# Loading and transposing half of the next x tiles during the second product, two blocks ahead

## The chip, the cores and the metric

The kernel runs on one core of a Trainium2 chip. The metric is the device time of one execution in microseconds (us). Each time below is a median over several executions. Verdicts are ratios with a 95% interval: the mean time of one kernel's fast runs over the mean of the other's fast runs in the same rounds, so not quite the ratio of the quoted medians.

## The reference, cut to what matters

```python
batch, m, k, h, n = 16, 512, 768, 3072, 768
y = np.matmul(x, w1) + b1                      # "first product"
y = 0.5 * y * (1.0 + erf(y / np.sqrt(2.0)))    # gelu
return np.matmul(y, w2).astype(np.float32)     # "second product"
```

The 8192 rows of x are worked off in 8 blocks of 1024 rows, numbered 0 to 7. A block has 8 row tiles of 128 rows.

## The kernel before

The kernel replaces 8 block multiplications by 7 (a Strassen scheme), twice nested in the second product. From block 2 on, every block is 12 "units" of the first product and 7 "units" of the second, each unit with seven products. Four parts matter here.

From block 2 on, all loads that the tensor engine waits for go through the queue of the sync engine (SP), in program order: first-layer weights (`w1s`, 672 KB a unit), second-layer weights into a ring of ten buffers (`w2s`, 288 KB a product), and the transposes of x (SBUF to SBUF). The loads of x go through the GpSimd (POOL) queue, with most stores of the output.

```python
def load_ring(sb, n):                    # second-layer weights of product n
    if n < 49 and sb < nsb:
        nc.sync.dma_start(out=ring_of(sb, n), in_=w2s[w2_order[n]][:])

def xh_of(sb, t):
    ...                                  # from block 2 on: three buffers for loaded x tiles
    return xh_late[t % 3]

def load_x(sb, t):
    xhs[t] = xh_of(sb, t)
    nc.gpsimd.dma_start(out=xhs[t], in_=xr[:, sb * 8 + t, :])

def transpose_dma(sb, t):
    nc.sync.dma_start_transpose(out=xT_of(sb, t), in_=xhs[t])

class Unit3:                             # a unit of the second product
    def mm(self, q, dst, first, c0, c1, ts=(0, 1)):
        n = w2_at[self.p, q]
        w = ring_of(self.sb, n)
        ...                              # 12 matmuls of 192 columns with w
        load_ring(self.sb, n + RING)     # RING = 10: refill the buffer just used
```

Between the products of a unit, "fill" functions issue everything else. This is the one of the first product (`k` is the unit, `slot` the place in it):

```python
def fill_mm1(sb, k, slot):
    ...
    if slot == 3 and sb + 1 < nsb:
        if 1 <= k < 9:
            load_x(sb + 1, k - 1)
        if 3 <= k < 11:
            transpose_dma(sb + 1, k - 3)
    if slot == 5:
        if k + 3 < NH and n + 3 not in wts:
            load_wt(n + 3)               # first-layer weights, three units ahead
        if k >= 3:
            for m in range(2 * (k - 3), min(2 * (k - 2), RING)):
                load_ring(sb, m)         # the first ten of the ring
```

The transposed x has two buffers, for even and odd blocks. So block `sb + 2`'s buffer is free as soon as block `sb`'s first product is done.

## Time and profile before

Median 855.0 us of six executions (854.53 to 856.19).

| what | number | view |
|---|---|---|
| tensor engine (PE) busy | 845.9 of 854.0 us | page, part 1 |
| granted clock | 0.999 | cores |
| one first-product unit, unstalled | 4.53 us | timeline, from start to start |
| one second-product unit, unstalled | 6.93 us | timeline |
| one block, unstalled | 12 x 4.53 + 7 x 6.93 = 102.9 us | |

The page of the kernel before: busy time of each engine, DMA share in 40 slices, and the chain of work that ended last.

```profile
PE 845.9 (99%) x6407; PEld 566.5 (66%) x6407; DVE 667.5 (78%) x1128; ACT 423.9 (50%) x688; POOL 83.7 (10%) x135
...
DMA  9996987659989698996989889897998969967397
...
PE 96%; DMA 3%; POOL 0%; issue 0%; DVE 0%
```

The tensor engine is the limit, and the DMA engines are nearly as busy. PE busy alone would not say that the matmuls run at their best rate. The unit times do: 4.53 us / 21 = 215.7 ns for a matmul of 512 columns, which is the 215.7 ns that the Trainium skill, page "TensorE: Matmul & The Clock Gate", section "Wait — 56ns, not 53.3ns?", gives for back-to-back matmuls of this size. So nothing but the few DMA pieces of the chain can be gained. One of them, in block 3's first product (chain in order of time: start, length, what):

```profile
371.52 1.25 PE bX L379 x6
372.77 9.93 DMA arena<-w1s
382.70 0.05 issue
382.75 0.82 PE bX L379 x3
```

The piece is as long as the load took from issue to landing (9.93 us). The tensor engine did not stand that long: it worked on earlier units for most of it, and the start-to-start gaps show 1.33 us of stall here and 0.33 us at 376.

The windows view of before by stage; after the times come the busy time (and count) of PE, PEld, DVE, ACT and POOL, then the granted clock, the DMA share and GB/s. The rows are block 3's first product, block 3's second, block 4's first, block 4's second.

```profile
343.00:397.30 54.30, 52.96 (x306) 28.07 (x304) 39.06 (x75) 39.52 (x62) 2.66 (x5) 1.00 0.95 241
397.30:445.00 47.70, 47.70 (x527) 43.73 (x525) 44.78 (x69) 11.02 (x21) 6.01 (x9) 1.00 0.91 326
446.00:500.30 54.30, 54.30 (x314) 29.06 (x313) 39.58 (x76) 40.65 (x64) 3.13 (x6) 1.00 0.94 254
500.30:548.00 47.70, 47.70 (x526) 43.75 (x525) 44.65 (x69) 10.42 (x21) 6.05 (x9) 1.00 0.91 320
```

Read the last two columns: both kinds of stage are above 0.9 in DMA share. The first product moves fewer GB/s at a higher share, because of small packets: in the first row the transposes (256 B, 35 ns a packet) and the x loads (1536 B, 148 ns) are 24% of the bytes and 45% of the packet time.

### The profile page before, as it was taken

To read this page: it belongs to the slowest core of one execution; us is meant where nothing else is said; L and a number is where in the kernel's file an instruction comes from. 1 tells how busy PE (TensorE), PEld (TensorE's weight loads), DVE (VectorE), ACT (ScalarE), POOL (GpSimd) and SP (SyncE) were. 2 spreads that over 40 slices of the span, in tenths; PEclk is the share of its full clock that TensorE was granted. 3 is DMA by queue.
4 is the path that set the end of the run, shared out by engine and by line. 5 is a ranking of instruction groups with operands and counts; after the bars stand their busy time and mean duration, and the time that the engine had idled before them with its cause. 6 is when DMAs were issued, how large, how long until landed. Compare 5 with 4: busy or idle time off the path is not lost.

```text
span 854.0 us, 16428 instructions
## 1 busy us (share of the span) xinstructions
PE 845.9 (99%) x6407; PEld 566.5 (66%) x6407; DVE 667.5 (78%) x1128; ACT 423.9 (50%) x688; POOL 83.7 (10%) x135
## 2 busy tenths in 40 slices
PE   8999999999999999999999999999999999999998
PEld 4444445687544897448974499645995469944798
DVE  5856678786657998669976799667996689957997
ACT  5777762122277513874138722477216771267611
POOL 5021100002100002000020000200012000010000
PEclk9999999999999999999999999999999999999999
DMA  9996987659989698996989889897998969967397
GB/s 226 235 232 89 256 165 269 240 194 216 234 225 291 212 321 293 265 287 228 333 287 271 254 275 334 274 339 158 313 347 264 307 170 333 348 218 266 101 304 286
DMA packets 143522, 219.05 MB, mean 256 GB/s; under 512 B 61756, under 2 KB 84724, under 8 KB 143444
## 3 DMA queue, kind: packets, MB, share of 16 engines
q1 hardware_dynamic: 117968, 179.83, 65.7%
q0 software_dynamic: 25440, 38.15, 21.1%
q8 instruction: 50, 0.82, 0.4%
q14 instruction: 28, 0.23, 0.1%
q10 hardware_dynamic: 36, 0.01, 0.0%
HBM read 180.30 MB, written 47.87 MB: 267 GB/s over the span
## 4 chain that ended last, share of the span: by engine, by line
PE 96%; DMA 3%; POOL 0%; issue 0%; DVE 0%
PE bY L379 21%; PE bY L484 15%; PE bX L379 14%; PE bX L484 10%; PE bZ L379 7%; PE bW L379 7%; PE bZ L484 5%; PE bW L484 5%; PE bY L423 5%; DMA arena<-w1s 2%; PE bZ L423 2%; PE bX L423 2%; PE bW L423 2%; DMA arena<-in_x_dram 1%; PE bY L571 1%; PE bX L571 1%
## 5 line engine op out<-in xcount | busy, mean ns | idle before, releaser
L189 DVE TENSOR_TENSOR arena<-arena 128x1536 f16<-128x1536 f16 (+7 forms) x632 | 403.5, 669 | 6.5 <-PE bW L423 1.1
L379 PEld LDWEIGHTS <-arena 128*128 128x128 f16 x1995 | 194.2, 98 | 229.6 <-DMA arena<-w1s 3.9
L484 PEld LDWEIGHTS <-arena 128*128 128x128 f16 x3528 | 292.1, 98 | 8.3 <-issue 0.3
L379 PE MATMUL bY<-arena 128*128 128x512 f16 x855 | 216.7, 379 | 0.0
L604 DVE TENSOR_TENSOR arena<-bY,arena 128x512 f32<-128x512 f32 (+1 forms) x103 | 70.1, 680 | 130.1 <-PE bY L379 89.6
L379 PE MATMUL bX<-arena 128*128 128x512 f16 x570 | 140.4, 379 | 1.5 <-DMA arena<-w1s 1.5
L597 ACT COPY bY<-bX 128x512 f32<-128x512 f32 (+1 forms) x144 | 79.2, 550 | 120.7 <-DVE arena L533 87.3
L484 PE MATMUL bY<-arena 128*128 128x192 f16 x1500 | 138.3, 246 | 0.0
L395 ACT ACTIVATE arena<-arena,b1t 128x1024 f16<-128x1024 f32 x95 | 109.2, 1149 | 54.8 <-DVE arena L632 54.8
L617 ACT COPY arena<-bW 128x512 f32<-128x512 f32 (+1 forms) x148 | 81.6, 552 | 91.5 <-PE bW L484 43.5
L484 PE MATMUL bX<-arena 128*128 128x192 f16 x1020 | 93.1, 246 | 0.0
L632 DVE TENSOR_TENSOR arena<-bZ,arena 128x512 f32<-128x512 f32 (+1 forms) x103 | 70.0, 679 | 22.8 <-PE bZ L379 18.8
L379 PE MATMUL bZ<-arena 128*128 128x512 f16 x285 | 77.0, 379 | 0.0
L379 PE MATMUL bW<-arena 128*128 128x512 f16 x285 | 77.0, 379 | 0.0
L423 PEld LDWEIGHTS <-arena 128*128 128x128 f16 x528 | 51.6, 98 | 34.1 <-issue 0.2
L400 ACT ACTIVATE arena<-bX,b1t 128x512 f16<-128x512 f32 x95 | 64.7, 681 | 10.4 <-PE bX L379 10.3
L516 POOL DMA_DIRECT2D out_dram<-arena x42 | 30.6, 728 | 395.1 <-DVE arena L628 358.6
L400 ACT ACTIVATE arena<-bY,b1t 128x512 f16<-128x512 f32 x95 | 64.0, 674 | 0.0
L648 ACT COPY bZ<-bY 128x512 f32<-128x512 f32 (+1 forms) x54 | 29.0, 537 | 65.5 <-DVE arena L632 30.5
L294 POOL DMA_DIRECT2D arena<-in_x_dram x60 | 32.5, 546 | 260.9 <-DMA arena<-arena 152.9
L650 DVE COPY bZ<-bY 128x512 f32<-128x512 f32 (+1 forms) x63 | 43.5, 691 | 6.3 <-DVE arena L632 0.5
L484 PE MATMUL bZ<-arena 128*128 128x192 f16 x504 | 48.5, 246 | 0.0
(60 smaller groups left out, 392.3 us busy)
## 6 DMA issues: line engine op xcount, KB each, us to landing
arena<-w2s SPq DMA_DIRECT2D x294, 288.0 KB, 4.7
arena<-w1s SPq DMA_DIRECT2D x72, 672.0 KB, 6.4
out_dram<-arena POOLq DMA_DIRECT2D x42, 384.0 KB, 5.4
w2s<-arena SPq DMA_DIRECT2D x49, 288.0 KB, 3.1
arena<-in_x_dram POOLq DMA_DIRECT2D x60, 192.0 KB, 6.8
w1s<-arena SPq DMA_DIRECT2D x12, 672.0 KB, 8.1
arena<-in_w_dram POOLq DMA_DIRECT2D x17, 384.0 KB, 8.5
out_dram<-arena SPq DMA_DIRECT2D x17, 384.0 KB, 3.4
```

Of the source, the lines that this page charges most:

```text
L189: nc.vector.tensor_tensor(out=o, in0=a, in1=b, op=op)
L294: nc.gpsimd.dma_start(out=xhs[t], in_=xr[:, sb * 8 + t, :])
L379: nc.tensor.matmul(out=dst[:, 0:RH], lhsT=w1_op(self.wt, slot)[:, c, :], rhs=a[:, c, :], start=first and c == 0, stop=c == self.C - 1, ski ...
L395: nc.scalar.activation(out=self.G[1][:, hi, :, :], in_=self.tmp, func=GELU, bias=b1t[:, 2 * hi + 1:2 * hi + 2])
L400: nc.scalar.activation(out=self.G[0][:, hi, row, :], in_=bank[:, 0:RH], func=GELU, bias=b1t[:, 2 * hi:2 * hi + 1])
L423: nc.tensor.matmul(out=dst[:, 0:N2], lhsT=a, rhs=w[:, :, c, :], start=first and c == 0, stop=c == self.C - 1, skip_group_check=True)
L484: nc.tensor.matmul(out=dst[:, t * N4:(t + 1) * N4], lhsT=a, rhs=w[:, c, :], start=first and c == 0 and t == ts[0], stop=c == NQ - 1, skip_ ...
L597: nc.scalar.copy(out=bY[u.g % 2][:, 0:u.F], in_=bX[u.g % 2][:, 0:u.F])
L604: nc.vector.tensor_tensor(out=u.c22(), in0=bY[u.g % 2][:, 0:u.F], in1=w[:, 0:u.F], op=ADD)
L617: nc.scalar.copy(out=w[:, 0:u.F], in_=bW[:, 0:u.F])
L632: nc.vector.tensor_tensor(out=u.c12(), in0=bZ[:, 0:u.F], in1=w[:, 0:u.F], op=ADD)
L650: nc.vector.tensor_copy(out=bZ[:, 0:u.F], in_=bY[u.g % 2][:, 0:u.F])
```

## The change

Its evident intent is to take DMA work out of the first product, where weights arrive late. For blocks 4 to 7, tiles 0 to 3 are loaded and transposed during the second product two blocks back, and tiles 4 to 7 stay in the first product at every other unit. Block 3 is fed as before.

```diff
             if slot == 3 and sb + 1 < nsb:
-                if 1 <= k < 9:
-                    load_x(sb + 1, k - 1)
-                if 3 <= k < 11:
-                    transpose_dma(sb + 1, k - 3)
+                ts = range(8) if sb == ONE else (4, 4, 5, 5, 6, 6, 7, 7)
+                if 1 <= k < 9 and (sb == ONE or k % 2):
+                    load_x(sb + 1, ts[k - 1])
+                if 3 <= k < 11 and (sb == ONE or k % 2):
+                    transpose_dma(sb + 1, ts[k - 3])
@@ the second product's fill @@
+            if sb + 2 < nsb and slot == 4:
+                if k < 4:
+                    load_x(sb + 2, k)
+                if 2 <= k < 6:
+                    transpose_dma(sb + 2, k - 2)
```

## The prediction

> **What bounds the kernel.** TensorE. The page gives PE 845.9 us busy of 854.0 (99%), the chain of waits is 96% PE, the granted clock is 0.999. By the timeline a first-product unit takes 4.53 us (21 matmuls of 512 columns) and a second-product unit 6.93 us (84 of 192), so a block needs 12 x 4.53 + 7 x 6.93 = 102.9 us. Blocks 4 to 6 take 102.97 to 103.15 us: nothing is left to gain there. Block 3 takes 104.68. The chain has two pieces "DMA arena<-w1s" of 9.8 and 9.9 us, one in block 2 (258.9, before the changed part), one in block 3 (372.8 to 382.7). Gaps between matmul starts in block 3 are 0.33 us at 376 and 1.33 us at 381: 1.7 us, for late first-layer weights. That is all the change can win.
>
> **What it moves.** Sixteen tiles (4 each for blocks 4 to 7) go from the first product of the block before to the second product two blocks back. No matmul, vector or scalar work changes. Per tile the trace shows a load (128 packets of 1536 B, 134 ns each under load: 1.1 us of all 16 DMA engines) and a DMA transpose (768 packets of 256 B, 18 to 19 ns alone, up to 79 ns crowded: 0.9 to 1.5 us), and 1.2 us of the SP queue.
>
> **First product.** The windows view gives DMA share 0.95 in block 3's first product, 0.93 to 0.94 in later ones. Weight loads there land 7 to 10 us after issue. Half the transposes, at every other unit, relieves this: I expect block 3's 1.7 us gone. The three x buffers come free early, so three of the four moved loads should issue near the end of the first product, where DMA is nearly idle (before: nothing at 488 to 492 us).
>
> **Second product.** This is the risk. DMA share is 0.90 to 0.91, but 0.96 to 1.03 in the middle units: a 288 KB ring load per 0.99 us product (0.75 us of DMA when packets take 93 ns) plus stores. A ring load is issued when product n ends and is needed 9 products later, 8.9 us. Its latency is 3 to 5 us, with a peak of 5.8 to 6.9 in unit 3 (blocks 2 to 5). Transposes come in units 2 to 5. The first should be absorbed; the second, with the fourth tile's load, adds 2 to 2.6 us just at the peak, the third about 1. Latency should reach 8 to 9.5 us: up to about 1 us of stall per block, in four blocks. I estimate 0 to 4 us, most likely 1.5.
>
> The Trainium skill, page "DMA: Bandwidth & Descriptors", section "Issuing engines are not separate DMA queues", says that all issuers end on the same 16 engines and interleave; the trace agrees (weight loads slow beside x loads and transposes), so moving work shifts it only.
>
> **Sum.** -1.7 + 1.5: about 855.0 us, range 852.8 to 859.5. Faster by over 2% is practically excluded, as PE idles under 1%; slower by over 2% would need over 4 us of stall in each of four blocks.
>
> **What would show it.** Right: no "w1s" piece at 372 us in the chain; block 3 at 103.0 us; DMA share of the changed first products about 0.8, second products near 1.0; ring loads (arena<-w2s) landing 2 to 3 us later in units 3 and 4. Wrong: PE waiting for arena<-w2s by several us per block.
>
> **What would make it wrong.** Transposes costing ring loads more than 1.5 us each; an in-order SP queue held by a transpose whose x load is late; first-product weights still late in block 3.

## The result, and the profile after

856.52 us median (855.54 to 858.19) against 855.0 us. The ratio is 1.0019, interval 1.0006 to 1.0032. Executions over 1.5% slower than the fastest of the same kernel are left out of the means. Two more sets of the same kernel, below, gave 1.0017 (0.9992 to 1.0042) and 0.9999 (0.9984 to 1.0014). So by the three ratios the change costs something between nothing and two tenths of a per cent (the widest interval reaches 0.42%), and two of the three sets cannot tell it from zero.

The same lines of the page after:

```profile
PE 845.8 (99%) x6407; PEld 566.3 (66%) x6407; DVE 667.8 (78%) x1128; ACT 423.3 (50%) x688; POOL 83.7 (10%) x135
...
DMA  9995987659999899986999789996999939967397
...
PE 95%; DMA 4%; SPq 0%; ACT 0%; issue 0%; DVE 0%
```

The same four stages in the windows view after:

```profile
343.00:397.30 54.30, 54.30 (x313) 28.91 (x311) 39.59 (x76) 41.09 (x65) 2.68 (x6) 1.00 0.88 235
397.40:445.10 47.70, 47.70 (x526) 43.75 (x525) 44.77 (x69) 11.03 (x21) 6.55 (x10) 1.00 1.07 340
446.10:500.40 54.30, 54.30 (x314) 29.04 (x313) 39.60 (x76) 40.60 (x64) 2.57 (x5) 1.00 0.86 236
500.40:548.10 47.70, 46.99 (x522) 43.28 (x520) 44.75 (x69) 9.60 (x19) 5.69 (x9) 1.00 1.06 328
```

The first products fell from 0.95 and 0.94 to 0.88 and 0.86 in DMA share, the second ones rose from 0.91 to 1.07 and 1.06. (Packet times can overlap, so a share can exceed 1.) The piece at 372 us is gone from the chain, and another has come in the second product of block 4:

```profile
518.27 0.57 PE bY L484 x7
518.85 8.99 DMA arena<-w2s
527.84 0.05 issue
527.89 1.16 PE bZ L484 x12
```

A ring load is needed 9 products after its issue, 9 x 0.99 = 8.9 us. This one took 8.99 us and was issued about 0.5 us after its turn (the loads before the transpose left every 0.99 us, the last at 515.33, so its turn was 518.30), behind a transpose on the queue; the stall was 0.87 us. The waits of the SP queue for a DMA to land show a kind that is absent before. Its largest line in the total:

```profile
SPq L283 <- DMA arena<-w2s: 10.5, 21, 1.8
```

The columns are us in total, times and longest. The trace has the SP queue's DMAs, transposes included, use eight completion semaphores (the signals that a DMA has landed) in turn. So the ninth DMA may have to wait for the first to land; that this is the reason for these waits is inferred.

To see where the stalls lie without the noise of the start, I measure each block by the time from its first ring refill (the eleventh ring load) to that of the next block. Without stalls this is 102.97 us. It holds the second product of the one block and the first product of the next. Ring latency, from issue to landing, is taken over the same refills: the first ten loads of a block, issued in its first product, can take longer (up to 10.2 us before) and have more time.

| profile | 2 to 3 | 3 to 4 | 4 to 5 | 5 to 6 | 6 to 7 | largest ring latency, blocks 2, 3, 4, 5 |
|---|---|---|---|---|---|---|
| before | 104.68 | 102.97 | 102.99 | 102.97 | 102.98 | 6.4, 6.2, 6.9, 5.8 |
| after | 103.46 | 102.98 | 103.87 | 103.05 | 102.99 | 8.8, 7.9, 9.2, 8.0 |

The 1.71 us in the first row is a wait for first-layer weights, the 0.49, 0.90 and 0.08 in the second are waits for the ring: 1.7 us gained, 1.5 us paid. (Block 2's first product, which the change does not touch, stalled by 0.5 us in the one profile and by 1.8 us in the other. That is why the profiled span of the changed kernel is the longer one, 854.8 against 854.0, although this balance is slightly in its favour.)

### The profile page after: what moved, and what is told of

It is laid out like the page before. It is cut to its first block, busy times and chain, and to the rows that moved or that the text cites. A ratio compares the mean times of both kernels' runs of the same rounds, so it can differ in the third digit from the quotient of the medians.

```text
span 854.8 us, 16436 instructions
## 1 busy us (share of the span) xinstructions
PE 845.8 (99%) x6407; PEld 566.3 (66%) x6407; DVE 667.8 (78%) x1128; ACT 423.3 (50%) x688; POOL 83.7 (10%) x135
## 4 chain that ended last, share of the span: by engine, by line
PE 95%; DMA 4%; SPq 0%; ACT 0%; issue 0%; DVE 0%
PE bY L379 21%; PE bX L379 14%; PE bY L484 14%; PE bX L484 9%; PE bW L379 7%; PE bZ L379 7%; PE bY L423 5%; PE bZ L484 5%; PE bW L484 4%; DMA arena<-w2s 2%; PE bZ L423 2%; PE bW L423 2%; PE bX L423 2%; PE bY L571 1%; DMA arena<-w1s 1%; DMA arena<-in_w_dram 1%
## 5 line engine op out<-in xcount | busy, mean ns | idle before, releaser
L400 ACT ACTIVATE arena<-bX,b1t 128x512 f16<-128x512 f32 x95 | 64.7, 681 | 10.4 <-PE bX L379 10.3
```

The costliest lines, as they stand in the source:

```text
L400: nc.scalar.activation(out=self.G[0][:, hi, row, :], in_=bank[:, 0:RH], func=GELU, bias=b1t[:, 2 * hi:2 * hi + 1])
```

## The experiments

Theory A: both kinds of stage lie at the edge of a deadline of about 9 us (first-layer weights in the one, ring loads in the other), and the DMA engines' time for x uses up the margin wherever it is put. Rival B: not the DMA engines' time matters but the in-order SP queue, which stands while a transpose waits or is being issued. Rival C: the stalls are chance, and the change does nothing.

### The two kernels again

before_again:

> The kernel before, unchanged, to see how much the stalls of TensorE vary from run to run. Theory A (the change trades a first-product stall of 1.7 us in block 3 for second-product stalls of about 1.3 us, and the rest of the measured difference is spread): the block 3 stall for first-layer weights is there again, 1 to 2.5 us, no stall for ring loads; the stall in block 2's first product, which the change does not touch, differs from the 0.5 us of the first profile. Rival C (the block 3 stall itself is chance): it is absent or under 0.5 us. Time 855.0.

after_again:

> The changed kernel again. Theory A: no stall for first-layer weights in block 3, ring-load stalls of 0.5 to 3 us in all in the second products of blocks 2 to 5; time 856.5. Rival C: the ring-load stalls of 0.46 and 0.87 us are gone, and what differs lies before block 2's second product.

after_third:

> The changed kernel a third time, for the size of its small loss and for a third look at where it stalls. The two sets so far have it 0.19% and 0.17% slower, the second not clear of zero. Theory A (the second products of blocks 2 to 5 now lie at the edge, so a stall of 0.3 to 1 us comes in some block of some executions, as the first products' did before): largest ring-load latency 7.5 to 9.2 us in blocks 2 to 5 and 5.4 to 7.1 in blocks 6 and 7, stalls of 0 to 2 us in all there, last weight load of blocks 3 to 5 within 8 us, time 855 to 856.5 us. If the loss of the first set was chance: within 0.05% of before.

| profile | 2 to 3 | 3 to 4 | 4 to 5 | 5 to 6 | 6 to 7 | largest ring latency, blocks 2, 3, 4, 5 |
|---|---|---|---|---|---|---|
| before_again | 102.99 | 102.97 | 104.40 | 102.97 | 102.98 | 6.2, 6.6, 6.3, 5.9 |
| after_again | 102.98 | 102.97 | 102.99 | 102.96 | 102.99 | 8.0, 7.6, 8.2, 7.6 |
| after_third | 103.38 | 102.98 | 103.00 | 102.98 | 103.00 | 8.4, 8.0, 8.6, 7.8 |

Times: before_again 855.37 us (its own ratio to the kernel before, the same kernel, 1.0005, 0.9989 to 1.0021), after_again 855.34 us, after_third 855.13 us. The expectation for block 3 failed: the weight stall was not there, it was in block 5. The chain of before_again shows it, and the SP queue's timeline shows what stood before the load:

```profile
577.20 0.85 PE bX L379 x4
578.05 10.05 DMA arena<-w1s
588.10 0.05 issue
```

```profile
572.70 0.32 SPq L216 DMA_DIRECT2D arena<-w1s  x1
573.07 1.32 SPq L283 DMA_DIRECT2D arena<-w2s  x2
575.87 2.09 SPq L300 DMA_TRANSPOSE arena<-arena  x1
578.05 0.76 SPq L216 DMA_DIRECT2D arena<-w1s  x1
```

The first two columns are the start and the length of what stands on the queue: from 574.39 the transpose stood at its head, waiting for its x tile, which landed at 575.85. Then its issue took 2.09 us, and the weight load left 5.35 us after the one before it instead of 4.53.

So a stall in a given block is chance (C is right there: after_again has no ring stall, where A expected 0.5 to 3 us), but the margins are not. Every profile of the kernel before has ring latencies of at most 6.9 us in blocks 2 to 5, every profile of the changed one has 7.6 to 9.2. The stalls of the changed kernel in these blocks were 1.5, 0.0 and 0.4 us, all for the ring and none for first-layer weights in blocks 3 to 5. In before they were 1.7 and 1.4 us, all for first-layer weights. As for the time, after_third was to lie within 0.05% of before if the loss of the first set was chance. It does (0.01%), but its interval of 0.15% to either side does not decide it.

### half_only: the relief without the price

```diff
 # from the changed kernel (wrong result on purpose: tiles 0 to 3 of blocks 4 to 7 are stale)
-            if sb + 2 < nsb and slot == 4:
-                if k < 4:
-                    load_x(sb + 2, k)
-                if 2 <= k < 6:
-                    transpose_dma(sb + 2, k - 2)
```

> The changed first product alone: tiles 0 to 3 of blocks 4 to 7 are not loaded at all (a wrong result on purpose), the others at every other unit. Theory A: the block 3 stall is gone and no ring-load stall appears, so 1.7 us below before: 853.3 us. If the relief is worth nothing, 855.0.

Measured: 854.52 us (853.98 to 854.75, the narrowest spread of all), ratio 0.9995, 0.9980 to 1.0010. Its block times are 102.99, 102.97, 102.98, 102.97 and 102.99: no stall at all. The mechanism is as expected; its worth is not. In the same rounds the kernel before had a median of 854.46 us (853.4 to 857.4). So the average execution hardly loses 1.7 us to late weights: the point estimate is 0.4 us, and 1.7 us lies at the edge of the interval. That the relief takes away slow executions rather than moving the median is what the two spreads suggest; six executions do not show it. The run leaves out loads and transposes together, so which of the two gives the relief was not tested.

### add_transposes and add_loads: which of the two costs

```diff
 # from the kernel before, in the second product's fill: add_transposes
+            if sb + 2 < nsb and slot == 4 and 2 <= k < 6:
+                xhs[k - 2] = xh_of(sb + 2, k - 2)
+                transpose_dma(sb + 2, k - 2)
 # ... and add_loads
+            if sb + 2 < nsb and slot == 4 and k < 4:
+                load_x(sb + 2, k)
```

> The kernel before with four more transposes (of old x tiles, overwritten later by the right ones) in units 2 to 5 of the second products of blocks 2 to 5, no loads moved. Theory A: the block 3 stall of 1.7 us stays and ring-load stalls of 0.5 to 2 us in all are added: about 856.3 us. If it is the x loads that push the ring loads late, no ring-load stall: 855.0.

> The kernel before with four more loads of x (of the tiles the change moves, loaded again later) at the places of the change, no transposes moved. Theory A: a load is 1.1 us of all DMA engines but in a queue of its own, and three of the four come free to issue before the second product's heavy part: largest ring-load latency 6 to 7.5 us, no ring-load stall, 854.5 to 855.5 us. If loads cost the ring as much as transposes, 7.6 to 9 us as in the changed kernel.

| run | time, us | ratio | largest ring latency, blocks 2, 3, 4, 5 | block times, us |
|---|---|---|---|---|
| add_transposes | 854.84 | 1.0003 (0.9985 to 1.0021) | 8.2, 7.9, 8.4, 7.6 | 103.78, 102.96, 103.28, 102.97, 102.99 |
| add_loads | 855.66 | 1.0000 (0.9972 to 1.0028) | 5.8, 6.4, 6.1, 6.1 | 103.75, 102.97, 104.58, 102.96, 102.98 |

Block 3's second product in the windows view, first in add_transposes, then in add_loads (it was 0.91 before and 1.07 after):

```profile
397.30:445.00 47.70, 47.70 (x517) 43.07 (x516) 43.58 (x67) 12.20 (x23) 7.19 (x11) 1.00 1.05 332
```

```profile
397.30:445.00 47.70, 47.70 (x519) 43.16 (x517) 43.71 (x67) 12.09 (x23) 7.08 (x11) 1.00 0.92 320
```

The transposes alone bring the ring latencies and the DMA share of the changed kernel; the loads alone leave both as before. (Without transposes to wait for, all four loads can go out early. A load exactly at the peak was not tried.) What stalls there are in either run are waits for first-layer weights in blocks 3 and 5, as in the kernel before. No time differs from before. The expected ring stalls of 0.5 to 2 us did not come in this profile of add_transposes: a latency of up to 8.4 us is still in time.

### twice_apart and double_transposes: the dose

```diff
 # from the changed kernel: double_transposes (the same destination twice; added behind the changed kernel's own call)
+                if 2 <= k < 6:
+                    transpose_dma(sb + 2, k - 2)
 # ... and twice_apart (the second into the tile that is written later anyway)
+                if 2 <= k < 6:
+                    nc.sync.dma_start_transpose(out=xT_of(sb + 2, k + 2), in_=xhs[k - 2])
```

> The changed kernel with each moved transpose issued twice in a row (same data, right result). Theory A: 0.9 to 1.7 us more DMA time four times a block; the margin is used up, so ring-load stalls of 2 to 5 us in each of blocks 2 to 5 and none elsewhere: 862 to 876 us. If the second products had room after all, under 858 us.

> The changed kernel with each moved transpose issued twice, the second into another place (overwritten later), so that the second does not wait for the first to land, as it did in the earlier double run: the doubled DMA work without that wait. Theory A: four more transposes of 0.9 to 3 us each in a stage with a few us to spare: ring-load latency over 8.9 us in each of blocks 2 to 5, stalls of 2 to 6 us a block, 863 to 880 us. If the 72 us of the earlier double run came from DMA work and not from that wait, about 925 us.

twice_apart: 880.33 us, ratio 1.0289 (1.0266 to 1.0313), correct. Block times 107.19, 112.03, 112.50, 107.22 and 103.00: 27 us over the unstalled ones (the time is just above the 863 to 880 us expected), or 1.7 us for each of the 16 added transposes, where the first 16 cost 0 to 1.5 us in all. Its waits of the tensor engine and one piece of its chain:

```profile
PE bY L484 <- DMA arena<-w2s: 17.6, 4, 6.5
```

```profile
417.34 0.99 PE bY L484 x12
418.33 0.01 PE bW L484
418.34 12.04 DMA arena<-w2s
```

This is what the spare room of the second product is: four transposes a block fit, eight in this arrangement do not. It fits A, but does not exclude B. The load of 418.34 took 12.04 us to land, and it also left 3.0 us after its turn (the last one before the two transposes left at 414.40, its turn was 0.99 us later). In block 4's stall the queue gave 4.3 us, with a latency of 11.02 us.

Nor are the 27 us all waiting. The gaps between matmul starts sum to some 18 us. Most of the rest is a lower clock: around the end of each of the four gaps of 2.6 to 6.7 us the trace grants the tensor engine half its clock, for 3.4 to 10.2 us. The windows view right after the gap of block 3 (the clock is the third number from the right):

```profile
430.40:436.30 5.90, 5.87 (x39) 5.59 (x40) 2.72 (x4) 0.48 (x1) 0.00 (x0) 0.52 1.13 329
```

After the changed kernel's own stalls, 0.9 us at most, the clock stays at 1.00. So stalls of a few us cost more here than their length.

double_transposes was a failed design that taught something else. It took 927.9 us (ratio 1.0846, 1.0817 to 1.0875), far above what A expected. The second transpose writes what the first writes, so it has to wait for the first to land, and the SP queue stands meanwhile:

```profile
307.81 1.80 SPq L283 DMA_DIRECT2D arena<-w2s  x4
309.71 11.77 SPq L300 DMA_TRANSPOSE arena<-arena  x2
321.57 3.38 SPq L283 DMA_DIRECT2D arena<-w2s  x7
```

For 11.77 us no ring load left the queue. The same number of transposes without that wait is 47.6 us faster (880.33 against 927.9). (Some 11 of the 47.6 us are again matmuls at the lower clock.) So B is a real mechanism, and in this pair the dearer one: a wait at the head of an in-order queue delays everything behind it.

### after_on_act: another queue

```diff
-                    transpose_dma(sb + 2, k - 2)
+                    nc.scalar.dma_start_transpose(out=xT_of(sb + 2, k - 2), in_=xhs[k - 2])
```

> The changed kernel with the moved transposes issued by the scalar engine's queue, so that the queue of the ring loads is not held; the DMA engines do the same work. Theory A (the DMA engines' time delays the ring loads): largest ring-load latency in blocks 2 to 5 stays at 7.5 to 9.5 us. Rival B (the in-order SP queue, held 1.2 to 1.7 us by each transpose, delays them): it falls to 5.8 to 7 us and the ring loads are issued every 0.99 us again.

Measured: 896.35 us, two of four executions slow; the fast ones (885.71 and 891.41) give a ratio of 1.0383 (1.0336 to 1.0431). Neither theory expected this. The profile is of a slow execution, so it is read only for what stands where, and its times are marked. The DMA view, with the median from issue to landing in its last column, has the other transposes, most of them of the first products, on SP and the moved ones on ACT:

```profile
arena<-arena SPq DMA_TRANSPOSE x38, 5.7
arena<-arena ACTq DMA_TRANSPOSE x16, 10.3
```

The two lines are of different stages. Like with like, the moved transposes landed after 7.1 us on SP in the changed kernel (median of the 12 whose landing the trace gives) and after 10.3 us here, and the ring loads beside them took up to 16.4 us (9.2 in the changed kernel). From first to last packet a moved transpose lasted 2.2 to 10.8 us here and 0.7 to 3.9 us in the changed kernel; why is not known. And the SP queue was not free of them. Its waits have a line that shows its ring loads standing until a moved transpose had landed, once for 8.4 to 12.2 us in each of blocks 2 to 5 and twice for 1.7 us (slow execution):

```profile
SPq L283 <- DMA arena<-arena: 41.6, 6, 12.2
```

The moved transposes take their turn in the same eight completion semaphores, which fits these waits; that this is the reason is inferred. So both premises failed, "the DMA engines do the same work" and "the queue of the ring loads is not held", and the run does not tell A from B.

### late_transposes and early_transposes: other places

```diff
 # late_transposes: after the last ring load; tile 3 in the next first product's unit 0
 # (cut: its transpose there, and the loads of tiles 0 to 2, placed as in the change)
+                if k == 6 and slot in (2, 3, 4):
+                    transpose_dma(sb + 2, slot - 2)
+                if k == 6 and slot == 5:
+                    load_x(sb + 2, 3)
 # early_transposes: before the output stores of unit 3
 # (cut: the loads of tiles 0 to 2, all three moved to k == 0, slot == 1)
+                for t, at_ in enumerate(((0, 3), (1, 2), (1, 5), (2, 3))):
+                    if (k, slot) == at_:
+                        transpose_dma(sb + 2, t)
+                if k == 0 and slot == 4:
+                    load_x(sb + 2, 3)
```

> The changed first product, but the moved transposes of tiles 0 to 2 come in unit 6 of the second product, after the last ring load, and tile 3 is loaded there and transposed in unit 0 of the next first product. Theory A (both stages lie at the edge of a deadline of about 9 us, and DMA work beside the ring loads or beside the first-layer weights uses up the margin): largest ring-load latency in blocks 2 to 5 back at 5.5 to 7 us (7.6 to 9.2 in the changed kernel), last weight load of blocks 3 to 5 landing within 8 us (9.0 to 10.3 before where it stalled), no stall of either kind there, time as with the tiles left out: 854 to 855 us with a narrow spread. Theory A fails if stalls over 0.3 us remain in blocks 3 to 5.

> The changed kernel with the four moved transposes earlier in the second product: in units 0, 1, 1 and 2, so all before the two output stores that come at unit 3. Theory A (what stalls is a ring-load latency over 8.9 us, built up where transposes meet the stores): largest ring-load latency in blocks 2 to 5 falls from 7.6 to 9.2 us to 6 to 8, no ring-load stall, no stall for first-layer weights in blocks 3 to 5; 854 to 855 us with a narrow spread. If it is only the amount of DMA work in the second product that counts, latencies of 8 to 9 us and stalls as in the changed kernel.

late_transposes: 865.56 us, ratio 1.0108 (1.0071 to 1.0145). The ring latencies are back at 5.7 to 6.2 us, as expected, but the block times are 103.98, 103.82, 107.42, 109.66 and 102.98. The chain shows why, around the start of block 5's first product:

```profile
540.31 5.56 DMA arena<-in_x_dram
545.87 0.02 issue
545.89 2.31 SPq L300
548.20 0.05 issue
548.25 7.07 DMA arena<-w1s
```

The load of tile 3 left only at 540.31, behind output stores on the POOL queue. The transpose of tile 3 stood at the head of the SP queue until 545.89 for it, and the weight load behind it left 9.3 us after the one before, where the kernel before issues the two 0.47 us apart. That is rival B again, of my own making. By the letter of its expectation theory A fails here, as stalls over 0.3 us remain in blocks 3 to 5; but these stalls have a cause that it had not reckoned with, so the run tests it only in the second product's latencies.

early_transposes: 858.62 us, ratio 1.0053 (1.0035 to 1.0071), the opposite of what was expected. The largest ring latency is 9.1 to 9.2 us in each of blocks 2 to 5, and each of the four periods loses 1.1 to 1.5 us (104.43, 104.09, 104.32, 104.21). So it does not take the stores of unit 3 to reach the deadline. A reading that fits is that four transposes within some 15 us build up a backlog that the ring loads cannot drain (0.75 us of DMA for each 0.99 us of product), while one in each unit of 6.93 us, as in the change, can just be borne. It was not tested apart from the time for which these transposes held the queue (1.2 to 3.6 us each).

### weights_first: the first product without moving anything

```diff
-                if 3 <= k < 11:
-                    transpose_dma(sb + 1, k - 3)
             if slot == 5:
                 ...                                  # load_wt and load_ring
+                if sb + 1 < nsb and 3 <= k < 11:
+                    transpose_dma(sb + 1, k - 3)
```

> The kernel before, nothing moved between blocks; each transpose is only issued after that unit's weight load and ring loads instead of before them (two fill slots later). Theory B for the first product (the last weight load is late because the in-order SP queue stands at a transpose that waits for its x tile; the load left 0.8 us late in both profiles that stalled): weight loads issued every 4.53 us in blocks 2 to 6, stalls for them under 0.3 us a block, 854 to 855 us. Theory A for the first product (it is the DMA engines' load alone, which stays the same): weight loads still land 9 to 10 us after issue and stalls of 1 to 1.7 us are there in one or two blocks.

Measured: 854.32 us, ratio 0.9992 (0.9979 to 1.0006): the same as before. Block times 103.58, 103.39, 102.99, 102.98 and 102.99 still show stalls of 0.6 and 0.4 us, and the last weight load of block 3 took 9.59 us to land:

```profile
372.38 9.59 DMA arena<-w1s
```

But the edit did not do what it was made for: weight loads still left late, up to 6.4 us after the one before in block 4, because the transposes still held the queue. So it does not tell A from B. The profile of add_transposes does, in part. In its block 3 all seven weight loads left on time, 4.51 to 4.55 us apart, and the last was late all the same, with a stall of 0.8 us:

```profile
371.26 10.26 DMA arena<-w1s
```

In add_loads it is the same in blocks 3 and 5: the last seven weight loads left 4.53 us apart, and the last took 10.2 and 11.06 us, for stalls of 0.8 and 1.6 us:

```profile
578.12 11.06 DMA arena<-w1s
```

A held queue is therefore not needed for a weight stall in the first product; where it is held, as in before_again, it comes on top. How much each gives is not settled.

No version beat both kernels clear of noise.

## Why the prediction was right or wrong

The time was right: 855.0 predicted (852.8 to 859.5), 856.5 measured in the first set and 855.1 to 855.3 in the later ones, and "within 2%" was what came. The range would also have held a change without any effect, and that -1.7 and +1.5 came out to the tenth is one draw: the other two profiles of the changed kernel paid 0.0 and 0.4 us.

1. **"That is all the change can win", 1.7 us in block 3.** Failed as a statement about a place and a worth. The weight stall wanders: block 3 in the first profile, block 5 in the second, both in add_loads. Taking the cause away altogether (half_only) gave a ratio of 0.9995, not clear of no effect. One profile of a kernel at the edge shows one draw.
2. **The relief of the first product.** Right in kind, and smaller than predicted: DMA share fell to 0.86 to 0.88 (about 0.8 was predicted). As expected, the last weight load of blocks 3 and 5 lands after 5.9 to 7.4 us instead of 8.3 to 10.1 (for block 4 the trace does not tell it), and no profile of the changed kernel has a weight stall in blocks 3 to 5.
3. **Three of the four moved loads leave early.** Right: in block 3 they were issued at 373.1, 381.0 and 381.5 us, before the second product.
4. **0.9 to 1.5 us of DMA per transpose.** Mis-sized. The packet times of the 16 moved transposes sum to 0.9 to 3.3 us of all 16 engines, 2.0 on average. (The prediction's own 79 ns for a crowded packet gives 768 x 79 / 16 ns = 3.8 us, not 1.5.) A transpose alone is 0.9 us; what it costs among other traffic cannot be read from it.
5. **The fourth tile's load adds to the peak.** Not supported. Transposes without any load bring the same latencies.
6. **Ring latency of 8 to 9.5 us, up to about 1 us of stall a block, 0 to 4 us in all, most likely 1.5.** Right: 7.6 to 9.2 us, at most 0.90 us a block, and 1.5, 0.0 and 0.4 us in all. Too small a transpose and a load that did not count, the errors of points 4 and 5, worked against each other, so that the size came out right partly by luck.
7. **Moving the work only shifts it.** Right for the latencies, which fell in the one stage and rose in the other. That the time moves so little is also because each of the two effects is small, 0.2% of the time at most in these profiles.

What stays open: why the weight stalls of the unchanged first product were seen in blocks 3 and 5 and never in 4 and 6 (weights_first, with another order of issue, stalled in 3 and 4), how much of a late load is the held queue and how much the DMA engines, in both products, and what part of the first set's 0.19% is the change.

## What to carry to other kernels

When the tensor engine is 99% busy and two stages both keep the DMA engines above 0.9, moving transfers from one to the other can trade waits and gain nothing, as here; first compare, in both stages, the latency of the loads with their deadline. Four transposes a block fitted into the second product for 0 to 1.5 us in all, and four more cost 27 us (a third of it matmuls at a lower clock after the stalls), so such room has to be measured by a dose, not read from the busy share. Do not put a transfer that must wait for another into the queue of loads that have a deadline: the waits cost more here (47.6 us in one pair) than the transfers.

## What the Trainium skill lacked or had wrong

- Page "DMA: Bandwidth & Descriptors", section "Issuing engines are not separate DMA queues", says that starting DMAs on several engines only saves the sequencer's time for issuing. The runs do not show this wrong, but it lacks a warning that doing so can also cost time: 16 transposes moved from the SP queue to the ACT queue made the fast executions 3.8% slower than before. In a slow execution they landed after 10.3 us (7.1 on SP in the changed kernel, both medians), and the SP queue's ring loads stood 41.6 us in six waits for them.
- The same page's section "DMA Transpose (X-bar)" gives no time for a transpose, and none beside other traffic. By its packets a 128 x 768 transpose of 2-byte elements took 0.9 us of all 16 DMA engines when alone and 2.0 us on average beside ring loads, and 1.2 us on the issuing queue at the least (2.09 us in before_again).
- The same page gives no figure for what a transpose that waits at the head of an issuing queue does to the loads behind it. Here one that had to wait for another to land held the queue for 11.77 us with its partner (double_transposes).
